# Moving the wait for the last stores into a second critical section that only SP enters

## The chip, the cores and the metric

One core of a Trainium2 chip (trn2) runs the kernel. Time is device time in microseconds (us) of one execution. A single execution of a one-core kernel has no second die to be compared with; the runs used here are those labelled fast, that is, within 1.5% of the fastest of the same kernel. Engines: DVE (VectorE), ACT (ScalarE), POOL (GpSimd), SP (SyncE), PE (TensorE, idle here). A view is one answer of the profile reader, and its lines are shown as they stand ("..." marks lines left out). A "q" after a name, as in SPq, is that engine's sequencer, which executes waits, signals, drains and branches.

## The reference

A 2x2 average pooling with stride 2 over `x` of 32 x 128 x 256 x 256 float32:

```python
output[:, :, i, j] = np.mean(x[:, :, 2*i:2*i+2, 2*j:2*j+2], axis=(2, 3))
```

So 1073.74 MB are read once, 268.44 MB are written once, and there is little arithmetic.

## The kernel before

All of it stands in one hand-synchronised section, `tc.tile_critical()`. Inside, each engine has its own stream: SP and ACT load the two halves of each input block, DVE adds rows and then columns, ACT multiplies by 0.25, POOL stores. SP and ACT store the last blocks, and every one of these last stores adds 16 to one semaphore, `tail`. The parts that the argument touches:

```python
    def take(engine, sem, n=1):
        engine.wait_ge(sem, n)
        engine.sem_inc(sem, -n)

    with tc.tile_critical():
        ...                                   # SP: all its loads
        store_from(sp, pairs - 1, c, tail)    # SP: two stores of 2 MB
        ...                                   # DVE: all its adds
        ...                                   # ACT: loads, scales
        act.dma_start(out=block(last, TILE)[1], in_=res[(whole - 1) % 4]).then_inc(tail, 16)
        for a, b, _ in parts:                 # two parts, the last stores, 1 MB each
            take(act, summed)
            scale(dst[:, a:b], done)
            take(act, done)
            act.dma_start(out=block((whole * TILE + a) * P, b - a)[1], in_=dst[:, a:b]).then_inc(tail, 16)
        ...                                   # POOL: all other stores
        pool.drain()
        take(sp, tail, 16 * (len(parts) + 3)) # SP: all five last stores have landed
```

The framework puts code around such a section. On leaving it SP signals, the other engines that were in it drain and signal back, and SP waits for them; after the last section, all five engines meet twice at a barrier, with a clearing of semaphores in between.

## Time and profile before

| | before |
|---|---|
| time, median of the first 3 runs | 3101.67 us (3101.55 to 3104.33) |
| profiled execution: time, span of its instructions | 3104.58 us, 3102.8 us |
| DMA | 1342.20 MB, share 1.00 of 16 engines, 433 GB/s |
| busiest engine | DVE, 54% |
| last store: issue, landing | 3093.18, 3101.64 us |
| from the tail wait's start to the end of the span | 1.155 us |

The page is read from the top: no engine is near full, the DMA row is. The kernel is bound by transfers for 3093 us, and then come the flight of the last store and about a microsecond of sequencer steps. The lines are shown in the prediction. Where this document gives times to a nanosecond, they are from the trace's records of single instructions and semaphore increments; the views print tenths.

### The profile page before, as it was taken

The page shows a single profiled execution, that of the slowest core. Times are in us where ns is not written, and L with a number is a line of the kernel's source. Part 1 is how long each engine was busy: PE and PEld are TensorE (multiplying, and loading weights), DVE is VectorE, ACT ScalarE, POOL GpSimd, SP SyncE. Part 2 cuts the span into 40 slices and gives each one's busy share as a digit, 9 for nine tenths or more (in the row PEclk, how much of TensorE's full clock was granted, in tenths as well). Part 3 has the DMA queues.
Part 4 walks back from the last instruction along what each step waited for, and adds up shares of the span by engine and source line. Part 5 has one row for each costly group of instructions (what it writes and reads, how often), then busy time and mean ns, then how long its engine had stood idle before and what let it go on. Part 6 is the DMA issues. An engine that isn't in the chain of part 4 may idle for free. (4 is left out here: it accounts for less than half of the span.)

```text
span 3102.8 us, 2903 instructions
## 1 busy us (share of the span) xinstructions
DVE 1679.2 (54%) x258; ACT 503.0 (16%) x160; POOL 67.5 (2%) x128
## 2 busy tenths in 40 slices
DVE  5555655556555565555655556555555555555555
ACT  1111112111121111211111111111111111111111
POOL 0000000000000000000000000000000000000000
DMA  9999999999999999999999999999999999999999
GB/s 419 427 438 433 438 427 439 430 433 435 438 427 439 434 430 433 432 436 436 436 429 439 433 433 433 439 426 433 439 435 430 439 426 434 437 433 433 439 430 403
DMA packets 31152, 1342.20 MB, mean 433 GB/s; under 512 B 6192, under 2 KB 6192, under 8 KB 6192
## 3 DMA queue, kind: packets, MB, share of 16 engines
q10 hardware_dynamic: 10752, 541.07, 40.3%
q1 hardware_dynamic: 10480, 541.07, 40.3%
q0 software_dynamic: 9920, 260.05, 19.4%
HBM read 1073.74 MB, written 268.44 MB: 433 GB/s over the span
## 5 line engine op out<-in xcount | busy, mean ns | idle before, releaser
L108 DVE TENSOR_TENSOR in_tile<-in_tile 128x8192 f32<-128x8192 f32 x129 | 1112.8, 8626 | 1393.0 <-DVEq L79 1393.0
L119 ACT ACTIVATE res<-res 128x4096 f32<-128x4096 f32 x127 | 459.4, 3617 | 1846.6 <-ACTq L79 1827.3
L110 DVE TENSOR_TENSOR res<-in_tile 128x4096 f32<-128x4096 f32 x127 | 562.0, 4425 | 18.6
L119 ACT ACT_TABLE_LOAD x31 | 39.8, 1283 | 735.5 <-ACTq L79 735.5
L132 POOL DMA_DIRECT2D out_dram<-res x124 | 67.3, 543 | 2941.7 <-POOLq L79 2939.0
L119 ACT ACTIVATE in_tile<-in_tile 128x2048 f32<-128x2048 f32 x2 | 3.8, 1910 | 8.0 <-ACTq L79 8.0
L110 DVE TENSOR_TENSOR in_tile<-in_tile 128x2048 f32<-128x2048 f32 x2 | 4.6, 2292 | 0.3
L287 POOL MEMSET const-float32-0.0<- 128x1 f32 x1 | 0.1, 93 | 0.4 <-issue 0.4
L287 POOL MEMSET const-bfloat16-1.0<- 128x1 bf16 x1 | 0.1, 97 | 0.0
L287 POOL MEMSET const-float32-1.0<- 128x1 f32 x1 | 0.1, 93 | 0.0
L287 POOL MEMSET const-uint8-127<- 128x1 uint8 x1 | 0.1, 93 | 0.0
## 6 DMA issues: line engine op xcount, KB each, us to landing
out_dram<-res POOLq DMA_DIRECT2D x124, 2048.0 KB, 42.2
in_tile<-in_x_dram ACTq DMA_DIRECT2D x2, 2048.0 KB, 21.9
in_tile<-in_x_dram SPq DMA_DIRECT2D x2, 2048.0 KB, 25.1
out_dram<-res SPq DMA_DIRECT2D x2, 2048.0 KB, 33.2
out_dram<-res ACTq DMA_DIRECT2D x1, 2048.0 KB, 14.4
out_dram<-in_tile ACTq DMA_DIRECT2D x2, 1024.0 KB, 10.1
in_tile<-in_x_dram SPq DMA_DIRECT2D x127, 32.2
in_tile<-in_x_dram ACTq DMA_DIRECT2D x127, 30.9
```

What stands on the lines that cost most here:

```text
L108: dve.tensor_add(out=it[:, :, 0:w], in0=it[:, :, 0:w], in1=it[:, :, w:]).then_inc(halfway)
L110: dve.tensor_add(out=dst, in0=it[:, :, 0:w:2], in1=it[:, :, 1:w:2]).then_inc(summed)
L119: act.mul(out=dst, in_=dst, mul=0.25).then_inc(sem)
L132: engine.dma_start(out=op[o][k], in_=src).then_inc(landed, 16)
L287: nc = _bacc.Bacc("TRN2", target_bir_lowering=False, num_devices=1)
```

## The change

The intent: the engines' meeting at the exit of the section should take place while the last stores are still in flight, and only SP should stay behind for them.

```diff
         pool.drain()
 
 
+    with tc.tile_critical():
         take(sp, tail, 16 * (len(parts) + 3))
```

## The prediction

> **What bounds the kernel now.** I read the head of the page first (busy shares, DMA row, totals of the queues), then a table of windows over the whole run and over its end, then what SP waits for, and last the instructions that the tile framework puts at the end of the critical section and of the program. The page's first section and its DMA totals:
>
> ```profile
> DVE 1679.2 (54%) x258; ACT 503.0 (16%) x160; POOL 67.5 (2%) x128
> DMA packets 31152, 1342.20 MB, mean 433 GB/s; under 512 B 6192, under 2 KB 6192, under 8 KB 6192
> HBM read 1073.74 MB, written 268.44 MB: 433 GB/s over the span
> ```
>
> No engine is busy for more than 54% of the span, and the bytes are exactly the input (1073.74 MB) read once and the output (268.44 MB) written once. The rest of the time is explained by transfer alone: 1342.2 MB at 433 GB/s is 3100 us, out of a span of 3102.8 us. The windows say the same by stage (columns: window, its length, then busy time of DVE, ACT and POOL with counts, clock, busy share of the DMA engines, GB/s):
>
> ```profile
> 500.00:1000.00 500.00, 275.46 (x42) 79.84 (x26) 10.84 (x20) 1.00 1.00 433
> 2500.00:3000.00 500.00, 272.00 (x42) 81.21 (x26) 10.84 (x20) 1.00 1.00 433
> ...
> 3082.00:3093.00 11.00, 8.90 (x3) 3.74 (x2) 0.00 (x0) 1.00 1.00 430
> 3093.00:3099.00 6.00, 0.00 (x0) 0.08 (x1) 0.00 (x0) 1.00 0.82 348
> 3099.00:3101.60 2.60, 0.00 (x0) 0.00 (x0) 0.00 (x0) 1.00 0.05 22
> 3101.60:3102.90 1.30, 0.00 (x0) 0.00 (x0) 0.00 (x0) 1.00 0.00 0
> ```
>
> The DMA engines are saturated (share 1.00) until 3093 us. The change touches only what comes after the last store has been issued, so the rest of the reading is about the last ten microseconds. There the last store drains, for its last 2.6 us on less than one of the 16 DMA engines (share 0.05; one engine would be 1/16 = 0.06), and then 1.3 us pass with no transfer at all. The store itself, in the view of line 196, and SP's wait for it, in the view of SP's waits from 3050 us on:
>
> ```profile
> L196 ACTq DMA_DIRECT2D out_dram<-in_tile x2: 343/344/344, 3086.4 to 3093.2; - x2
> ...
> DMA to landing us min/median/max: 8.5/10.1/11.8
> ```
>
> ```profile
> SPq L79 <- SPq L79: 67.3, 3, 42.3
> ```
>
> ACT issues the last of the stores at 3093.18 us and it lands 8.46 us later, at 3101.64. SP has stood in the tail wait for 42.3 us by then (from 3059.36, when its own last store was issued) and its wait instruction starts at 3101.66. So this wait is truly the end of the work, and what follows it is framework code. The lines of the critical section's exit (line 142) and of the program's end (line 301):
>
> ```profile
> L142 SPq EVENT_SEMAPHORE  x3: 17/17/28, 3101.7 to 3101.9; - x3
> L142 SPq NOP  x2: 13/13/13, 0.9 to 3102.0; - x2
> L142 ACTq DRAIN  x1: 8/8/8, 3101.8 to 3101.8; - x1
> L142 POOLq DRAIN  x1: 34/34/34, 3101.8 to 3101.8; - x1
> L142 DVEq DRAIN  x1: 10/10/10, 3101.8 to 3101.8; - x1
> L142 SPq DRAIN  x1: 7/7/7, 3101.8 to 3101.8; - x1
> ```
>
> ```profile
> L301 SPq DRAIN  x3: 7/7/7, 3102.1 to 3102.4; - x3
> L301 POOLq EVENT_SEMAPHORE  x4: 17/17/17, 3102.2 to 3102.7; - x4
> L301 PEldq EVENT_SEMAPHORE  x2: 51/51/51, 3102.3 to 3102.8; - x2
> ```
>
> What to see: the exit of the section is a meeting of SP, ACT, POOL and DVE, all between 3101.7 and 3102.0, that is, all after the tail wait, although ACT, DVE and POOL had long been done. ACT's last instruction ended at 3093.5, DVE's at 3091.0, and POOL's explicit drain at 3074.2. Then come two all-engine barriers with a clearing of semaphores between them, 3102.1 to 3102.8.
>
> **What the Trainium skill says.** Four places bear on this. "Perfetto Trace Analysis", Per-engine timelines, Sequencer-only Instruction: the reported start of such an instruction is when its semaphores are satisfied, and the wait before it isn't in the record. The trace agrees: the tail wait is a record of 17 ns at 3101.66, 0.02 us after the last landing, not one of 42 us. "DMA: Bandwidth & Descriptors", Why a DMA increments its semaphore by 16 and not by 1: only the full count means that the data has landed. The code waits for 16 x (2 + 3) = 80, and the trace's semaphore records show the 80th increment at 3101.64. The same page, Anatomy of one DMA, gives a fit of 2.0 us plus bytes over 436 GB/s. In the window from 3093 to 3103 us the DMA view has 2.15 MB, so an estimate by that page is 2.0 + 4.9 = 6.9 us, against 8.46 measured; the trace decides, and the difference is about the thin end on under one engine. Nothing in this flight is changed. "Runtime: NRT & Kernel Launch", Instruction fetch mechanics: a taken branch to a page outside the fetched window stalls the engine. The trace shows no such stall where SP leaves the section (0.07 us between its NOP and its next DRAIN).
>
> **The change part by part.** It removes nothing from the work: the same wait for the same 80 increments is executed by SP. It adds a second section with one engine in it, and it moves the meeting of the four engines from behind the wait to before it. No load, store, add or scale is touched, nor the order of any issue, because SP's wait was already its last instruction of the section.
>
> Step 1, the flight of the stores: unchanged, so the wait still starts at 3101.66 us. Cost 0.
>
> Step 2, the first exit, now early. ACT comes last to it, after its last store issue (3093.53). Adding one drain and SP's waits of the exit (0.37 us from the first record of line 142 after the tail wait at 3101.725 to SP's next DRAIN at 3102.088) gives about 3093.9. Entry of the second section: at the start of the program the NOP, the branch and the first instruction in the section are at 0.86, 0.94 and 1.10, so 0.24 us. SP stands at the tail wait again by about 3094.2, and has 7.5 us to spare before 3101.66. Cost 0 on the path. POOL's drain at the exit might take long while DVE is working (its explicit drain took 10.2 us beside DVE's adds, whereas the one at 3101.8, with DVE idle, took 34 ns), but DVE ends at 3091.0, before ACT arrives, so this is hidden too.
>
> Step 3, what is left behind the wait. Before, SP's starts by the records of single instructions are 3101.659 (wait), .725 (signal to the others), .805 (drain), .884 and .942 (two waits for the others), 3102.014 (NOP, third wait), .088 (drain of the program's end), .152 (its second drain, which joins the barrier): 0.493 us. With SP alone I expect wait, drain, NOP, and the same two drains. By the same intervals (0.080 + 0.079 + 0.074 + 0.064, rounded) that is about 0.29 us. The gain is 0.20 us. If the signal stays it is 0.13; if the NOP goes as well, 0.28.
>
> Step 4, the end of the program: from SP's joining at 3102.152 to the end at 3102.814 there are 0.66 us of barrier, clearing, barrier. They must still come after SP, so they stay. Other engines arrive earlier, but POOL, which gathers, waits for SP as before. Gain 0.
>
> Sum: 0 + 0 - 0.20 + 0 = -0.20 us, 0.006% of the time. Even if all 1.15 us after the wait vanished, that would be 0.04%.
>
> **The rivals.** First, the second section's entry or its branch lands on the path, for instance by a meeting with all engines again or a stalled fetch behind the wait: against it speaks the 7.5 us of slack before the wait and the absence of a stall at the existing exit; for it only that a new block of code is there. It would make some +0.3 to +2 us (a guess in size). Second, the gain is nothing because the exit of a section with one engine keeps all of its steps with the other engines: then the time is the old one, 3101.7. Third, the whole tail of 1.15 us is hidden: this would need the final barrier to be finished without SP, but its drain is in that barrier, so 3100.5 is out of reach. Fourth, the repetitions: the four executions before took 3101.55, 3101.67, 3104.33 and (profiled) 3104.58, so there are two clusters 2.9 us apart, and which of them the median falls in outweighs the effect by 14 to 1. The steady state at share 1.00 and 433 GB/s can also differ by a little from chip to chip: 0.1% of the rate is 3.1 us. I think this fourth one sets the measured difference.
>
> **Range and chances.** The base is the median 3101.67; minus 0.20 is 3101.5 us. The range is not from the mechanism (-0.3 to +0.1) but from the repetitions: the upper cluster at 3104.5 has to be in it, and 2.5 us under the lowest run for another chip or a better interleaving of transfers, so 3099.0 to 3105.0. Two per cent would be 62 us, which is 54 times all that follows the tail wait. Chances: faster 0.005, within 2% 0.99, slower 0.005.
>
> **What would show the steps right or wrong.** Right: in the changed kernel's view by line, the drains of ACT, POOL and DVE at the exit stand at or before about 3093.6 us rather than 8 us later; SP has a second set of entry instructions near 3094; the store's flight is again near 8.5 us, of 80 increments; between the tail wait's start and SP's joining of the final barrier there are about 0.3 us, not 0.49; from there to the end still 0.66. Step 2 is wrong if any new instruction of SP stands between the landing and the wait; step 3 if the drains of the other engines still follow the wait; step 4 if the barrier's 0.66 us change. The prediction as a whole would be wrong if the steady windows' rate differed from 433 GB/s by more than 0.1%, for which I see no way from this edit except chance.

## The result

The changed kernel took 3102.87 us (median of 6 runs, 3101.32 to 3106.19), the one before 3101.75 us in the same rounds (6 runs, 3101.55 to 3104.33). The ratio is 1.0003, with a 95% interval of 0.999 to 1.0016: no difference that timing can show, and the medians have the opposite sign to the forecast. Ratios in this document are the mean time of one kernel's fast runs over that of the other's of the same rounds, so not quite the ratio of the quoted medians. The median is in the predicted range, 1.4 us above the predicted point.

The profiled span is 3102.1 us. The instructions of the exit of the first section (line 142 of the changed kernel), in the view by line; columns are line, engine, operation, count, duration in ns (min/median/max), first and last start in us:

```profile
L142 SPq EVENT_SEMAPHORE  x3: 17/17/2567, 3058.3 to 3090.6; - x3
L142 SPq NOP  x2: 13/13/13, 0.9 to 3093.2; - x2
L142 SPq DRAIN  x1: 306/306/306, 3058.4 to 3058.4; - x1
L142 POOLq DRAIN  x1: 34/34/34, 3073.7 to 3073.7; - x1
L142 DVEq DRAIN  x1: 2298/2298/2298, 3088.2 to 3088.2; - x1
L142 ACTq DRAIN  x1: 152/152/152, 3093.0 to 3093.0; - x1
```

Before, these all stood at 3101.7 to 3102.0, behind the landing. Now SP signals at 3058.3, as soon as it has issued its own stores, and each other engine drains where its own work ends: POOL at 3073.7, DVE at 3088.2 (queued behind its last add, hence 2.3 us), ACT at 3093.0. SP's last step of the meeting, the NOP, is at 3093.2, eight microseconds before the landing.

The instructions of the second section (line 210) and of the program's end (line 302, which was 301), in the same view of the changed kernel:

```profile
L210 SPq NOP  x2: 13/13/13, 3093.3 to 3101.4; - x2
L210 SPq EVENT_SEMAPHORE  x1: 17/17/17, 3101.2 to 3101.2; - x1
L210 SPq DRAIN  x1: 7/7/7, 3101.3 to 3101.3; - x1
```

```profile
L302 POOLq EVENT_SEMAPHORE  x4: 17/17/17, 3101.5 to 3102.0; - x4
...
L302 SPq DRAIN  x3: 7/7/7, 3101.4 to 3101.7; - x3
...
L302 PEldq EVENT_SEMAPHORE  x2: 51/51/51, 3101.6 to 3102.1; - x2
```

Behind the landing there remain a signal, a drain and a NOP of SP alone, and the same closing barriers. The flight of the last store, in the view of line 196 of the changed kernel, and the end by windows (columns as in the prediction's window table):

```profile
L196 ACTq DMA_DIRECT2D out_dram<-in_tile x2: 343/343/343, 3085.9 to 3092.6; - x2
...
DMA to landing us min/median/max: 8.5/10.3/12.1
```

```profile
3092.60:3099.00 6.40, 0.00 (x0) 0.00 (x0) 0.00 (x0) 1.00 0.80 339
3099.00:3101.10 2.10, 0.00 (x0) 0.00 (x0) 0.00 (x0) 1.00 0.05 20
3101.10:3102.20 1.10, 0.00 (x0) 0.00 (x0) 0.00 (x0) 1.00 0.00 0
```

The flight is 8.51 us (8.46 before) and ends on the same thin remainder at share 0.05. Only the empty stretch behind it is shorter. Step by step, from the start of the tail wait (it starts 0.02 us after the last landing in both), by the records of single instructions:

| start, us after the tail wait's | before | changed |
|---|---|---|
| SP signals | 0.066 | 0.079 |
| SP drains | 0.146 | 0.158 |
| SP waits for the others | 0.225, 0.283 | - |
| SP's NOP (before: also waits for POOL) | 0.355 | 0.231 |
| first drain of the program's end | 0.429 | 0.275 |
| second drain, which joins the barrier | 0.493 | 0.339 |
| POOL gathers | 0.525 | 0.371 |
| end of the span | 1.155 | 1.001 |

So the mechanism works and is worth 1.155 - 1.001 = 0.154 us. The column "before" is one profile; the same exit in one of the experiments below (eight meetings behind the wait) has its steps up to the NOP at 0.066, 0.146, 0.231, 0.289 and 0.356 us, within 0.006 us of it. The two profiled spans differ by 0.67 us, because the tail wait also starts 0.52 us earlier; that part arose in the stream of transfers (the 127th large add of DVE starts at 3064.23 before and 3063.67 in the changed kernel), where the two kernels have the same code.

### The profile page after: what moved, and what is told of

The parts are those of the page before. It is cut to its first block, busy times and chain, and to the rows that moved or that the text cites. A ratio compares the mean times of both kernels' runs of the same rounds, so it can differ in the third digit from the quotient of the medians.

```text
span 3102.1 us, 2910 instructions
## 1 busy us (share of the span) xinstructions
DVE 1679.2 (54%) x258; ACT 502.9 (16%) x160; POOL 67.5 (2%) x128
```

## The experiments

The theory: the change moves the exit's meeting off the end of the path and gains about 0.15 us; what the timings show beyond that is scatter of the stream. Rivals: the second section costs something of its own (the first medians, 1.1 us apart, could be read so); a meeting costs nothing anyway; or it costs its time wherever it stands. Nine runs were made, of the changed kernel twice more and of seven other kernels, on three chips. All gave correct results.

**The changed kernel again.** No edit.

> The changed kernel itself again, more repetitions. My theory (the meeting of the engines moved off the end, worth 0.15 us, and the rest is chance): from the start of SP's tail wait to the end of the program again 1.00 us (1.155 before the change), and ratio to before 0.9995 to 1.0005, with runs of both kernels spread over some 3101.3 to 3106. Rival (the second section disturbs something and costs about 1 us, which the first medians would say): its runs lie again above those of before, median by 1 us or more.

From the tail wait to the end: 1.001 us again. Time 3101.41 us median of the five fast runs, 3101.36 the lowest; before, in the same rounds, 3104.35 and 3101.51; ratio 0.9988 (0.9966 to 1.0009; one run of 3193.44 was slow and left out). This time the median of the kernel before is the higher one, by 2.9 us. The rival that the section costs a microsecond falls; nothing in the two kernels' tails explains which median is higher.

**Eight more meetings behind the wait.** In the kernel before:

```diff
         take(sp, tail, 16 * (len(parts) + 3))
+    for _ in range(8):
+        with tc.tile_critical():
+            for engine in (sp, act, dve, pool):
+                engine.drain()
```

> The kernel before with eight more sections of four engines (each drains) behind the tail wait, so eight more meetings on the path. Theory (a meeting costs where it stands on the path: entry, some 0.24 us, and exit, some 0.42 us, by the traces): from the tail wait to the end 1.155 + 8 x 0.66 = 6.4 us instead of 1.155, and the kernel longer by some 5.3 us, ratio 1.0017. Rival (the framework's meetings overlap or cost next to nothing, so that the change could not have gained anything): under 2.5 us in all.

From the tail wait to the end: 8.03 us, so (8.025 - 1.155) / 8 = 0.86 us for each section, not 0.66. By line, the sections' instructions all stand behind the landing at 3121.8 (columns as above):

```profile
L213 SPq NOP  x16: 13/13/13, 3122.3 to 3129.1; - x16
L213 POOLq DRAIN  x8: 34/34/34, 3122.7 to 3128.9; - x8
...
L213 ACTq DRAIN  x8: 8/8/132, 3122.9 to 3128.8; - x8
```

From one section's branch to the next it is 0.74 to 0.76 us where nothing interferes, and up to 1.11 us where SP shows a gap of 0.42 us without any instruction. The direction is right, the size was underestimated: a meeting does cost its time when it stands on the path. Five of the six runs are between 3111.28 and 3111.91 us, the lowest 9.8 us above the lowest of before (3101.51), which is 2.9 us more than the profiled tail explains. In the profile the flight of the last store was 9.63 us too, 1.17 us longer than before; if the timed runs had that as well, 1.7 us stay unexplained. The ratio, 1.002 (0.9999 to 1.0041), is blurred by scatter of both kernels (the sixth run has 3131.49, the highest of before 3120.79).

**The same eight meetings ahead of the wait.** In the changed kernel, between the two sections:

```diff
+    for _ in range(8):
+        with tc.tile_critical():
+            for engine in (sp, act, dve, pool):
+                engine.drain()
     with tc.tile_critical():
         take(sp, tail, 16 * (len(parts) + 3))
```

> The changed kernel with the same eight sections of four engines between its first section and SP's own, so in front of the tail wait, in the flight of the last store. Theory (7.6 us of slack before the landing hide them): they take some 5.3 us from 3093.2 on, SP stands at the tail wait by about 3099, the wait still starts about 8.5 us after the last store's issue, from it to the end 1.00 us, ratio to before 1.000. Rival (a meeting costs its time wherever it stands): longer by 5.3 us, ratio 1.0017.

The sections' NOPs on SP and SP's tail wait (last start) in the views of line 211 and line 79 of this kernel:

```profile
L211 SPq NOP  x16: 13/13/18, 3095.2 to 3102.0; - x16
```

```profile
L79 SPq EVENT_SEMAPHORE  x128: 17/17/17, 39.3 to 3104.1; - x128
```

They run from 3095.2 to 3102.05 us, SP branches into its own section at 3102.31, and the tail wait starts at 3104.14, 0.017 us after the last landing. From there to the end 1.014 us, against 8.03 with the same sections behind it: 7.0 us of the tail are hidden by position (0.15 of them are the gain of the change itself, since the other run started from the kernel before). Not as expected was the flight, 9.60 us instead of 8.5; see below. The timings would not have shown any of this: ratio 1.0000 (0.9978 to 1.0021), but the median of the five runs is 3106.74 us (lowest 3102.53), 5.3 us above that of the changed kernel in the same rounds, which is about what the rival forecast for the meetings. The profile, itself of a run of 3106.78 us, speaks against the rival: its tail wait starts 2.48 us later than in the kernel before, 1.34 of that arose in the stream by the 127th add and 1.14 in the flight, and none in a meeting.

**Thirty meetings ahead of the wait.** The same with `range(30)`.

> As before, but thirty sections ahead of the tail wait: some 20 us, more than the slack. Theory: 7.6 us of them hidden, the rest, some 12 us, on the path, so the end 12 us later, ratio 1.004; SP's tail wait then starts long after the last landing. Rival (no limit to what is hidden): ratio 1.000. Rival (nothing hidden): 20 us, 1.0064.

The last store and SP's tail wait, in the views of line 196 and of line 79 of this kernel:

```profile
L196 ACTq DMA_DIRECT2D out_dram<-in_tile x2: 344/344/344, 3086.9 to 3093.6; - x2
...
DMA to landing us min/median/max: 9.7/10.6/11.5
```

```profile
L79 SPq EVENT_SEMAPHORE  x128: 17/17/17, 39.4 to 3118.8; - x128
```

The store was issued at 3093.62 and landed at 3103.31, but SP reached its wait only at 3118.84, 15.5 us later. The meetings took 3118.84 - 3094.25 = 24.6 us, 0.82 each; some 9 us of them lay in the flight and 15.5 us on the path (expected: 7.6 and 12). So what is hidden is what fits into the flight and no more. From the tail wait to the end it was 1.365 us here, not 1.00; 0.33 of the difference is a longer pause between two of POOL's steps in the closing barriers. The four runs are between 3121.84 (the profiled one) and 3130.45 us, and the ratio, 1.0074 (1.0048 to 1.01), lies above both forecasts, 1.004 for the theory and 1.0064 for "nothing hidden". So the time alone does not refute that rival; the 9 us of meetings that lie in the flight are read from the trace.

**Eight more sections of SP alone behind the wait.** In the changed kernel:

```diff
         take(sp, tail, 16 * (len(parts) + 3))
+    for _ in range(8):
+        with tc.tile_critical():
+            sp.drain()
```

> The changed kernel with eight more sections of SP alone (a drain each) behind the tail wait. Theory (a section of one engine still pays its own SP steps, some five to seven of 0.07 us: signal, drain, NOP, entry NOP, branch): 8 x 0.4 = 3.2 us, so from the tail wait to the end 4.2 us; less per section than in the sections of four engines (0.66 expected). Rival (a section of one engine is free, so all of the remaining 0.34 us before the barrier is something else): under 0.5 us. Rival (it costs as much as one of four): 5.3 us.

From the tail wait to the end: 6.45 us, so (6.451 - 1.001) / 8 = 0.68 us each, where 0.4 was expected. Undisturbed ones are 0.624 us apart. The count of steps was wrong. In the view by line the section's own instructions are four (two NOPs, a signal, a drain), but SP also executes two waits and a branch of the framework on entry and the drain in the body: eight steps, 0.05 to 0.16 us apart. Two of the view's three lines:

```profile
L214 SPq NOP  x16: 13/13/18, 3102.0 to 3107.4; - x16
L214 SPq EVENT_SEMAPHORE  x8: 17/17/17, 3102.4 to 3107.2; - x8
```

The theory failed here, and the rival that such a section costs as much as one of four engines (5.3 us in all) came nearest: 6.451 - 1.001 = 5.45 us. It is a useful correction: the cost of a section is mostly SP's own chain of steps (0.624 us), and the other engines add 0.739 - 0.624 = 0.115 us. Time 3108.48 us median, ratio 1.0052 (0.9994 to 1.0111; one of the four runs took 3151.40 us and still counts as fast). The lowest run, 3107.04, is 5.6 us above the lowest of before, 3101.46; the tails differ by 6.451 - 1.155 = 5.3 us in the traces.

**POOL waits instead of SP.** In the changed kernel:

```diff
     with tc.tile_critical():
-        take(sp, tail, 16 * (len(parts) + 3))
+        take(pool, tail, 16 * (len(parts) + 3))
```

> The changed kernel with the tail wait on POOL instead of SP, alone in the second section: POOL gathers the closing barrier, so one hop from SP to POOL goes. Theory (what is left behind the wait is a chain of sequencer steps of 0.06 to 0.08 us on whichever engine waits): from the tail wait to POOL's gathering step 0.35 to 0.45 us against 0.37 in the changed kernel, end within 0.1 us of it, ratio within the scatter. Rival (the hop is what matters): 0.1 us or more shorter.

From the wait to POOL's gathering step 0.421 us (0.371 with SP), to the end 1.053 us. The hop is saved, but POOL's own steps are longer (its drains 34 ns, SP's 7). Ratio 1.0019 (0.9986 to 1.0051). As expected; no gain this way.

**A finer last block.** In the changed kernel, the last 32 rows are cut 16+8+4+4 instead of 16+16:

```diff
-        b = rest if rest - a <= 16 else a + (rest - a) // 2
+        b = rest if rest - a <= 4 else a + (rest - a) // 2
```

> The changed kernel with the last block cut into 16+8+4+4 rows instead of 16+16, so the last stores are of 256 KB. Theory (the end is set by the flight of stores that the saturated engines still have to drain, not by the sections): the last issue comes earlier, by up to some 4 us, but the landing moves by less than 3 us, because the transfers are busy until about 3098; the distance from the landing to the end stays 1.00 us; ratio 0.999 to 1.0005. Rival (the last issue sets the landing): 3 to 4 us earlier, ratio 0.9988.

From the tail wait to the end 1.001 us again. This execution was 2.18 us late by the 127th large add (3066.41 against 3064.23). Set off against that, the last issue came 0.5 us earlier than before (3094.84 - 2.18 = 3092.66, against 3093.18), and the landing 0.3 us later (3104.10 - 2.18 = 3101.92, against 3101.64): the last store, a quarter as large, was 9.26 us in flight. Ratio 1.0011 (0.9977 to 1.0046). No gain; and since the issue moved by only 0.5 us instead of up to 4, it is a weak test of what sets the landing.

**ACT waits, in one section.** In the kernel before:

```diff
-        take(sp, tail, 16 * (len(parts) + 3))
+        take(act, tail, 16 * (len(parts) + 3))
```

> The kernel before, with one section only, but ACT instead of SP waits for the stores at its end. Theory (what counts is only which sequencer steps stand behind the landing; the second section is one way to move SP's signal and the other engines' drains ahead of it): SP signals at about 3059, DVE and POOL drain early, and behind the landing stand ACT's drain, SP's last wait, NOP and two drains: 0.25 to 0.33 us from ACT's wait to SP's joining of the barrier (0.34 in the changed kernel, 0.49 before), so 0.92 to 1.0 us to the end, without any second section. Rival (the gain needs the second section): 1.155 us to the end as before.

The exit of the only section, in the view by line of this kernel:

```profile
L142 SPq EVENT_SEMAPHORE  x3: 17/17/10622, 3061.5 to 3093.6; - x3
L142 SPq NOP  x2: 13/13/13, 0.9 to 3104.3; - x2
...
L142 POOLq DRAIN  x1: 34/34/34, 3076.7 to 3076.7; - x1
L142 DVEq DRAIN  x1: 2300/2300/2300, 3091.2 to 3091.2; - x1
L142 ACTq DRAIN  x1: 8/8/8, 3104.2 to 3104.2; - x1
```

SP signals at 3061.5 and POOL and DVE drain early, as in the changed kernel, without a second section. Behind the wait (3104.11) stand ACT's drain (+0.087 us), SP's NOP (+0.165) and two drains (+0.239, +0.303): 0.303 us to the joining of the barrier and 0.974 us to the end, 0.027 less than the changed kernel. The gain does not need the second section. What it needs is that SP's signal, which lets the others leave, does not stand behind the wait. Time 3102.2 us median, 3101.20 the lowest, ratio 0.9989 (0.997 to 1.0009). It has the shortest tail of all kernels run, and timing cannot tell it from the others.

**The changed kernel a third time**.

> The changed kernel a third time, on the chip of this call. Theory: 1.00 us again from the tail wait to the end; the lowest run lies 0.1 to 0.2 us under the lowest of before, all else is scatter of several us in both. Rival (the change costs about 1 us): lowest and middle run above those of before by 1 us.

Once more 1.001 us. But the profiled execution has a span of 3116.7 us: its tail wait starts at 3115.67. Two windows of the stream show where (columns as before):

```profile
1500.00:2000.00 500.00, 266.18 (x41) 82.35 (x26) 11.87 (x22) 1.00 1.00 433
...
2500.00:3000.00 500.00, 263.97 (x41) 82.35 (x26) 10.78 (x20) 1.00 1.00 428
```

The rate falls from 433 to 428 GB/s while the DMA engines stay fully busy. The 71st large add is 0.10 us behind that of the kernel before, the 101st 3.58, the 127th 14.06. The profile of eight meetings behind the wait was 19 us late by the 127th add too, and its code is the same up to there. Median 3105.26 us against 3103.99 of the ten fast runs of before, ratio 1.0002 (0.9977 to 1.0026; one run of before, 3151.04, was slow and left out). So the middle run lies 1.3 us above, as the rival said, and the lowest does not: the lowest runs were 3101.39 and 3101.40, only 0.01 us apart instead of the expected 0.1 to 0.2.

**A plain wait outside any section** (`take` in the framework's own scheduling) did not build: the framework found that the semaphore would drop below zero. It could not be tried as it stood.

**All timings together.** Over all rounds the kernel before has 38 fast runs, median 3102.60 us, and the changed one 17, median 3101.71 us (one slow run of each left out). Both come in a dense group below 3102.1 us (19 and 10 runs) and a long upper part. Within that group, chosen after the fact, the medians are 3101.68 and 3101.41, and the lowest runs 3101.40 and 3101.32. This agrees in sign with the 0.154 us of the traces, but it is not a measurement of it.

## Why the prediction was right

**Bound.** Right: the stream sets the time, with 433 to 435 GB/s and share 1.00 in both kernels' windows from 100 to 3000 us. The prediction's own sign of being wrong, a rate off by more than 0.1%, did appear in the third profile of the changed kernel (14.06 us late by the 127th add, 0.46%); but the kernel with eight meetings behind the wait, which has the code of the kernel before up to there, was 19 us late in its profile, so this lateness does not need the edit.

**Step 1, the flight unchanged.** Right: 8.51 and 8.52 us in two traces, 8.42 in the third, against 8.46.

**Step 2, the first exit early and hidden.** Right. SP's branch into the second section ended at 3093.54 (predicted about 3094.2), 7.6 us before the wait was satisfied; counted from the end of ACT's last issue that is 0.57 us where 0.67 was predicted. The entry had two more waits than I listed, 0.13 us, also hidden. The fear about POOL was unfounded: its exit drain took 34 ns while DVE was adding. The meetings ahead of and behind the wait show the principle at some 45 times the size: 7.0 us difference in the tail for the same sections, by position.

**Step 3, what is left behind the wait.** Right in mechanism, a little off in size: 0.339 us instead of about 0.29 (the sum shown there is 0.297), so a gain of 0.154 us instead of 0.20. The term is the signal, which I expected to go and which stayed (0.079 us); the prediction's own variant for that case, 0.13, is nearer. The NOP stayed, but the next drain, which no longer waits for a signal of it, followed sooner (0.044 us, not 0.074).

**Step 4, the closing barriers.** Right: 0.66 us from SP's joining to the end in both.

**Rivals.** The first, a cost of the second section on the path, is refuted for this kernel by three traces of 1.001 us. (The prediction sought its sign, a stall, at the existing exit; the record has SP's branch on entry, at 3093.50 us, and what follows it is hidden by 7.6 us of waiting.) The second, no gain, is refuted by the same traces. The third, all hidden, did not occur. The fourth, that repetitions outweigh the effect, is what the timings are: the sign of the difference of medians changed from the first (+1.1 us) to the second (-2.9 us) and back to the third (+1.3 us). I took the scatter for two clusters 2.9 us apart; with 39 runs of the kernel before it is a dense group at 3101.4 to 3102.0 and values up to 3109, with three at 3120 to 3123 and a slow one at 3151. That the first median lay in the range is therefore in part luck, and it says nothing of the mechanism: the range of 3099.0 to 3105.0 held the first median but would have missed a later median of the changed kernel, 3105.26. It was too narrow for that upper part.

**What stays open.** What lowers the rate in some executions is not settled. The views show the rate; the packet records add that some packets take longer: from 2500 to 3000 us the 64 KB packets of queue q10 took 2463 ns on average in the third profile of the changed kernel and 2418 in its first, with a median of 2418 in both. Nor is it known why kernels with eight or thirty additional four-engine sections have a flight of 9.6 to 9.7 us (8.4 to 8.5 in all others whose last store is of 1 MB), and why their timed runs exceed what the profiled tail explains. One thing in the DMA view bears on it: with sections ahead of the wait, four packets of 8 KB of a queue q14, kind "instruction", run during the last flight (3094.5 to 3104.2 us with eight, 3093.6 to 3103.4 with thirty); the kernel before has none in its own (3093.2 to 3101.7). But with eight sections behind the wait the flight was 9.63 us without any, in an execution that was late by 19 us; so these packets cannot be the cause in all three.

## What to carry to other kernels

The signal that lets the other engines leave should not stand behind the wait for the last stores: give the wait a section of its own, or give it to another engine. Then the others' meeting lies in the flight of the store, and only a short chain of steps remains. Judge such a change from the distance between the last landing and the end in the trace, which was 1.001 us from the tail wait on in all three profiles of the changed kernel, not from medians that scatter by several microseconds. And ask first what the whole tail is worth: 1.155 us of 3102, while the median of one and the same kernel moved by 2.6 us (3101.75 to 3104.38), so no rearrangement of that tail could have been seen in the time.

## What the Trainium skill lacked or had wrong

- "Perfetto Trace Analysis", Per-engine timelines, Sequencer-only Instruction: the wait is said to lie outside the record. That holds for SP's tail wait (17 ns after 42 us of waiting). It did not hold for SP's waits with two semaphores: records of 2.57 us (changed kernel), 10.62 us (ACT waits) and 8.11 us (POOL waits), which ended when the other engine came.
- No page gives the cost of a section of the framework: 0.62 us with one engine and 0.74 us with four, a drain in each included, where nothing interferes; both are mostly a chain of SP's steps, eight or ten of them, 0.05 to 0.16 us apart.
- "Runtime: NRT & Kernel Launch", Instruction fetch mechanics, has fetch stalls after a taken branch, without a duration. At a few places in the long chains of sections SP shows gaps of 0.33 to 0.44 us without any instruction. The six of them that lie behind the landing are each followed by an 8 KB DMA packet of kind "instruction", which starts 0.7 to 1.3 us after the gap began and after it had ended; so SP did not wait for that packet, and the cause of the gaps stays open.
- "DMA: Bandwidth & Descriptors" has nothing on how long a store issued by ACT takes behind a stream that fills the DMA engines; its fit, under Anatomy of one DMA, is for the gpsimd path. Here 1 MB took 8.4 to 9.7 us from issue to landing and 256 KB 9.26 us; in the kernel before, the last of the 80 increments came 2.43 us after the 79th.
